# RWKV recurrence: eight blocks of two heads, taken in four pairs

## The chip, the cores and the metric

One core of a Trainium2 chip runs the whole program in one launch. The metric is the device time of one execution in microseconds. TensorE (PE in the profile, its weight loads PEld) multiplies, VectorE (DVE) and ScalarE (ACT) copy and compute, GpSimd (POOL) fills buffers and takes powers, and SyncE (SP) issues the loads.

## The reference

A network of two blocks on 256 positions of width 1024. The change touches one of its parts, the RWKV time mix of the first layer:

```python
def wkv7_scan(r, decay, k, v, a, b):
    def step(S, inp):
        r_t, w_t, k_t, v_t, a_t, b_t = inp
        sa = jnp.einsum('bhij,bhj->bhi', S, a_t)
        S = S * w_t[:, :, None, :] + sa[..., None] * b_t[:, :, None, :] + v_t[..., None] * k_t[:, :, None, :]
        return S, jnp.einsum('bhij,bhj->bhi', S, r_t)
    _, y = lax.scan(step, S0, xs)

def rwkv7_time_mix(...):
    ...
    y = wkv7_scan(heads(r), heads(decay), heads(k), heads(v), -kk, kk * a_h)
    mean = jnp.mean(y, axis=-1, keepdims=True)
    var = jnp.mean(jnp.square(y - mean), axis=-1, keepdims=True)
    y = ((y - mean) * lax.rsqrt(var + RWKV_LN_EPS)).reshape(B, T, C) * ln_g + ln_b
    bonus = jnp.sum(heads(r) * heads(k) * r_k, axis=-1, keepdims=True)
    y = y + (bonus * heads(v)).reshape(B, T, C)
    return (y.astype(h.dtype) * g) @ w_o
```

There are 16 heads of width 64. Everything else (feed-forward layers, differential attention, the second block with its expert lookup) is the same in both kernels.

## The kernel before

Activations lie transposed, 128 channels on the partitions and 256 positions in the free dimension, in eight column blocks `d`. One `d` holds two heads of 64 channels; below, "head" means one `d`. The scan over 256 steps is done in two chunks of 128 positions, each as a triangular system.

Around the change the work goes so. While the value projection runs (`rproj`, whose matmuls are `mm<-xs,raw`), DVE solves small triangular systems (L659, L661), and `prep` builds for heads 0 and 1 what the chains need: four transposes into one bank (`tr`), copied to `tk`, and four grams (`gr`, L243) of 64 rows each, copied under a mask into `gm` (L1215). Then class `Wkv` runs one generator `head(d)` for each head. It copies the solved 32x32 blocks into block-diagonal buffers `xb` (L1234 on DVE for the first two heads, L1236 on ACT after that; eight copies a head), multiplies `lp` and `lx` to an inverse (`zt` copied under a mask at L1249, the result `x3`, shown as `x`, at L1256), and runs two chunks. A chunk is a chain in one bank `ch`: PE starts it (`ch<-tk,gm`), DVE copies half to `rt` (L1271), PE multiplies by the inverse (`ch<-rt,x`), DVE copies to `ut` (L1280), PE (`ch<-ut,xs`), DVE `rt` (L1287), PE, DVE `ut`, then the output (`ch<-gm`) that ACT copies to `y` (L1303), and after the first chunk the state `s0` (`sp`, L1302). The head's tail normalises `y` (`mn`, L1314, `smp`, POOL's power L336, four `yn` at L1323 to L1326), and `last_proj` multiplies by the output projection as heads become ready. Its first three blocks are added to `x` at L391; five more follow.

Three sets of `gm`, `zt` and `tk` exist (`nb` is 3), so head `d` waits until head `d-3` has ended. PSUM's banks are rings of `wk` (four), `sm` (two) and `mm` (two); the grams use `sm`, as does the statistics bank `smp`; `tr`, `lp`, `lx`, `ch`, `sp` and `mn` use `wk`. `stagger` starts a generator every five rounds, at most five at once. A scheduler under the language then sets each engine's order; each engine runs its own in order.

Of the kernel before, what the change touches and what calls it, by code (L numbers as in the profile page):

```python
# [173 lines left out]
class Net:  # L174
# [219 lines left out]
    def transposes(self, ins, out):  # L394
        p = self.wkt("tr")
# [764 lines left out]
class Wkv:  # L1160
    def __init__(self, net, ar, bt, kt, gg, vf, tab, xd, xtd, gram):
        self.net = net
        self.a = (ar, bt, kt, gg, vf, tab, xd, xtd, gram)
        self.gms, self.tks, self.zts, self.x1s, self.pre = [], [], [], [], {}
# [9 lines left out]
    def buffers(self, pool, s):  # L1174
        nc = self.net.nc
        gm = pool.tile([128, 4, 384], F32, name=f"gm{s}")
        z = pool.tile([128, 4, 128], F32, name=f"zt{s}")
        nc.gpsimd.memset(gm, 0.0)
        nc.gpsimd.tensor_copy(z, self.net.ident[:, None, :].to_broadcast([128, 4, 128]))
        self.gms.append(gm)  # L1180
        self.zts.append(z)
        self.tks.append(pool.tile([128, 4, 128], F32, name=f"tk{s}"))

    def diag(self, pool, s):
        x1 = pool.tile([128, 2, 4, 128], F32, name=f"xb{s}")
        self.net.nc.gpsimd.memset(x1, 0.0)
# [12 lines left out]

    def prep(self, d):  # L1200
# [167 lines left out]
```

## Time and profile before

| | |
|---|---|
| median of three runs | 2212.38 us (2208.43 to 2221.66) |
| profiled execution | 2211.49 us, span 2209.7 us |
| PE, PEld busy | 2169.1, 2032.6 us (98%, 92%) |
| DVE, ACT, POOL busy | 1533.2, 1116.3, 78.0 us |
| mean granted TensorE clock | 0.994 |
| first `lp` of the recurrence | 348.05 us into the span |
| last `y` copy | 454.44 us |
| first residual copy after the output projection (L391) | 465.33 us |

The recurrence proper is the stretch from 348 to 465 us, some 5% of the span. Busy PE is no measure of its work, since matmuls are pipelined and their ends are modelled; how soon the next instruction starts says more.

### The profile page before, as it was taken

The numbers are of one execution on the slowest core, as the hardware profiler recorded it, in microseconds if no ns is written. First come the engines' busy times: TensorE is split into PE (matmuls) and PEld (weight loads), VectorE is DVE, ScalarE is ACT, GpSimd is POOL, SyncE is SP. The second block draws the span as 40 slices with busy tenths as digits, with TensorE's granted clock in tenths as the row PEclk, the third lists the DMA queues.
The fourth block names the chain that finished last, engine by engine and source line by source line (L and its number), as shares of the span: only waits on it lengthen the run. The fifth ranks groups of instructions, "written<-read, shape, count | busy, mean of one in ns | idle before, by whom it ended". The sixth has DMA issues, their size and how long they took to land.

```text
span 2209.7 us, 40311 instructions
## 1 busy us (share of the span) xinstructions
PE 2169.1 (98%) x16048; PEld 2032.6 (92%) x16048; DVE 1533.2 (69%) x2982; ACT 1116.3 (51%) x2070; POOL 78.0 (4%) x109
## 2 busy tenths in 40 slices
PE   8999999989999999999999999999999999999999
PEld 8998777779999999989999999999999999888887
DVE  6665695666666666486666767999489985666665
ACT  5443633344454444475445654444576654554554
POOL 0000040000000000020001000000000000000000
PEclk9999999999999999999999999999999999999999
DMA  6564331135565555435565445555544345555554
GB/s 214 183 180 141 117 105 39 39 105 182 180 183 179 167 179 178 136 112 189 183 180 179 136 145 172 163 172 176 192 138 131 130 145 187 192 192 195 194 192 152
DMA packets 98589, 351.06 MB, mean 159 GB/s; under 512 B 10944, under 2 KB 12480, under 8 KB 98272
## 3 DMA queue, kind: packets, MB, share of 16 engines
q1 hardware_dynamic: 98400, 348.48, 49.2%
q8 instruction: 126, 2.06, 0.4%
q14 instruction: 63, 0.52, 0.1%
HBM read 347.38 MB, written 1.05 MB: 158 GB/s over the span
## 4 chain that ended last, share of the span: by engine, by line
PE 48%; DVE 5%; issue 1%; ACT 0%; DMA 0%; POOLq 0%; POOL 0%; ACTq 0%
PE mm L243 28%; PE y L243 16%; PE pg L243 3%; DVE wl L258 2%; DVE dm L1130 1%; DVE ex L1135 0%; PE sc L243 0%; DVE dm L1133 0%; PE po L243 0%; DVE v L1098 0%; PE tr L762 0%; PE psc L243 0%; DMA raw<-in_p_u_dram 0%; DVE si L1100 0%; PE smp L243 0%
## 5 line engine op out<-in xcount | busy, mean ns | idle before, releaser
L243 PE MATMUL mm<-xs,wh 128*128 128x256 f32 x6304 | 1160.4, 286 | 14.0 <-ACT wh L255 6.8
L243 PEld LDWEIGHTS mm<-xs,wh 128*128 128x128 f32 x6304 | 988.3, 193 | 20.4 <-ACT wh L255 6.8
L258 DVE TENSOR_TENSOR wl<-raw,wh 128x1024 fp32r<-128x1024 f32 (+1 forms) x633 | 765.9, 1210 | 328.0 <-ACT wh L255 327.0
L255 ACT ACTIVATE wh<-raw 128x1024 fp32r<-128x1024 f32 (+1 forms) x633 | 660.5, 1044 | 594.7 <-PE mm L243 472.5
L243 PE MATMUL mm<-xs,wl 128*128 128x256 f32 x3152 | 896.6, 285 | 2.0 <-DVE wl L258 2.0
L243 PEld LDWEIGHTS mm<-xs,wl 128*128 128x128 f32 x3152 | 607.2, 193 | 2.9 <-DVE wl L258 2.9
L243 PE MATMUL y<-wh,cs 128*128 128x512 f32 x1024 | 274.0, 390 | 0.0
L243 PE MATMUL mm<-hh,wh 128*128 128x256 f32 x1408 | 250.1, 281 | 0.0
L243 PEld LDWEIGHTS y<-wh,cs 128*128 128x128 f32 x1024 | 192.3, 188 | 39.6
L243 PEld LDWEIGHTS mm<-hh,wh 128*128 128x128 f32 x1408 | 215.9, 188 | 0.0
L243 PE MATMUL mm<-hh,wl 128*128 128x256 f32 x704 | 198.1, 281 | 0.0
L243 PE MATMUL y<-wl,cs 128*128 128x512 f32 x512 | 157.8, 390 | 0.0
L243 PEld LDWEIGHTS mm<-hh,wl 128*128 128x128 f32 x704 | 132.6, 188 | 0.0
L243 PE MATMUL mm<-xs,raw 128*128 128x256 f32 x512 | 126.1, 394 | 2.5 <-DVE xs L490 2.5
L243 PEld LDWEIGHTS y<-wl,cs 128*128 128x128 f32 x512 | 96.2, 188 | 20.0
L306 ACT ACTIVATE cs<-ga 128x256 fp32r<-128x256 f32 x103 | 43.0, 418 | 136.9 <-PE y L243 136.7
L243 PEld LDWEIGHTS mm<-xs,raw 128*128 128x128 f32 x512 | 96.2, 197 | 16.9 <-DVE xs L490 2.9
L420 DVE TENSOR_TENSOR gu<-mm,rstd 128x512 f32<-128x512 f32 x88 | 60.8, 691 | 44.4 <-PE mm L243 44.2
L306 ACT ACTIVATE hh<-hv 128x256 fp32r<-128x256 f32 x88 | 36.6, 416 | 104.6 <-DVE hv L425 104.6
L307 DVE TENSOR_TENSOR cs<-ga,cs 128x256 fp32r<-128x256 f32 x103 | 43.8, 426 | 55.1 <-ACT cs L306 55.1
L1045 DVE TENSOR_SCALAR ohb<-iota,xT 128x128 f32<-128x128 f32 x192 | 59.5, 343 | 15.3 <-PE pg L243 13.9
L243 PE MATMUL pg<-ohb,xT 128*128 128x128 f32 x512 | 65.9, 276 | 0.0
(320 smaller groups left out, 1883.9 us busy)
## 6 DMA issues: line engine op xcount, KB each, us to landing
raw<-in_ffn_in_dram SPq DMA_DIRECT2D x176, 512.0 KB, 3.8
raw<-in_p_u_dram SPq DMA_DIRECT2D x128, 512.0 KB, 3.7
raw<-in_p_v_dram SPq DMA_DIRECT2D x128, 512.0 KB, 4.3
raw<-in_ffn_out_dram SPq DMA_DIRECT2D x64, 512.0 KB, 3.6
raw<-in_w_in_dram SPq DMA_DIRECT2D x34, 512.0 KB, 3.7
raw<-in_ffn_out_dram SPq DMA_DIRECT2D x32, 384.0 KB, 3.3
raw<-in_w_rkv_dram SPq DMA_DIRECT2D x24, 512.0 KB, 3.7
raw<-in_w_kv_dram SPq DMA_DIRECT2D x16, 512.0 KB, 3.7
```

The costliest lines, as they stand in the source:

```text
L243: self.nc.tensor.matmul(out, lhsT, rhs, start=start, stop=stop, skip_group_check=True)
L255: hi = nc.scalar.activation(fh[:rows, :w], raw[:rows, :w], AF.Copy)
L258: lo = nc.vector.tensor_tensor(fl[:rows, :w], raw[:rows, :w], fh[:rows, :w].bitcast(F32), op=ALU.subtract)
L306: nc.scalar.activation(dst[rows, :T], src, AF.Copy)
L307: nc.vector.tensor_tensor(dst[rows, T:], src, dst[rows, :T].bitcast(F32), op=ALU.subtract)
L420: nc.vector.tensor_tensor(t, p.rearrange("p (a b) -> p a b", a=2), box["r"][:, None, :].to_broadcast([128, 2, T]), op=ALU.mult)
L1045: nc.vector.tensor_scalar(b, iota, itp[:, 1, t:t + 1], itp[:, 2, t:t + 1], op0=ALU.is_equal, op1=ALU.mult)
L1130: nc.vector.tensor_tensor(m, iota[:, None, :50].to_broadcast([128, 16, 50]), bf[:, h, :, None].to_broadcast([128, 16, 50]), op=ALU.is_equal)
```

## The change

Two heads go through one generator `pair(n)`. Each chain step writes both heads' columns of one bank (`p` the first 256 columns, `pu` the other), and one DVE copy of 256 columns moves them. The state's matmuls and the output reuse the same bank, and `sp` is gone. `front(d)` builds a head's inverse, now without waiting for an earlier head's end; `tail(d)` is the old tail, run for both heads in step. In `prep` the two halves' grams alternate in two banks. The inverse is kept as its two diagonal blocks of 64 (`x3` has 64 columns, two ACT copies). There are two `zt` and four `gm` and `tk`; the last two `tk` lie in a buffer `spare` taken from the ring of split weights. `tr`, `lp` and `lx` use `sm`.

```diff
-    def transposes(self, ins, out):
-        p = self.wkt("tr")
+    def transposes(self, ins, out, bank=None):
+        p = (bank or self.wkt)("tr")
...
     def run(self, yo, w_o):
-        for s in range(2, EVERY["nb"]):
-            self.buffers(lp, s)
+        spare = net.wp.tile([128, 8, 128], F32, name="spare", tag="wh")
+        for s in range(2, 4):
+            self.buffers(lp, s, spare[:, 4 * s - 8:4 * s - 4])
-        self.x3 = lambda: lp.tile([128, 4, 128], F32, name="x3", bufs=3)
+        self.x3 = lambda: lp.tile([128, 4, 64], F32, name="x3", bufs=4)
-        stagger([self.head(d) for d in range(8)] + [net.last_proj(w_o, yo, self.ready, True)], EVERY["wkv"], EVERY["width"])
+        stagger([self.pair(n) for n in range(4)] + [net.last_proj(w_o, yo, self.ready, True)], EVERY["wkv"], EVERY["width"])
     def prep(self, d):
-        yield from net.transposes([vf[:, d, :128], vf[:, d, 128:], bt[:, d, 0], kt[:, d, 0]], f2(tk))
-        for q in range(4):
-            hh, c = q // 2, q % 2
-            hs = slice(64 * hh, 64 * hh + 64)
-            p = net.smt("gr")
-            net.mm(p[:, :128], bt[hs, d, c], ar[hs, d, c, 1], True, False)
-            net.mm(p[:, 128:384], kt[hs, d, c], ar[hs, d, c].rearrange("p a b -> p (a b)"), False, True)
-            yield
-            nc.vector.copy_predicated(gm[:, q], gmask, p[:, :384])
+        yield from net.transposes([vf[:, d, :128], vf[:, d, 128:], bt[:, d, 0], kt[:, d, 0]], f2(tk), net.smt)
+        for c in range(2):
+            ps = [net.smt("gr") for hh in range(2)]
+            for part in range(2):
+                for hh, p in enumerate(ps):
+                    hs = slice(64 * hh, 64 * hh + 64)
+                    if part == 0:
+                        net.mm(p[:, :128], bt[hs, d, c], ar[hs, d, c, 1], True, False)
+                    else:
+                        net.mm(p[:, 128:384], kt[hs, d, c], ar[hs, d, c].rearrange("p a b -> p (a b)"), False, True)
+            yield
+            for hh, p in enumerate(ps):
+                nc.vector.copy_predicated(gm[:, 2 * hh + c], gmask, p[:, :384])
...
+    def front(self, d):
...
+        p = net.smt("lp")
...
+        p = net.smt("lx")
...
+        xc = self.x3()
+        for lo in (0, 64):
+            rows = slice(lo, lo + 64)
+            nc.scalar.activation(xc[rows], p[rows].rearrange("p (a b) -> p a b", a=4)[:, :, rows], AF.Copy)
+        self.solved.add(d)
+        yield
+        while d >= 4 and d - 4 not in self.ended:
+            yield
+        if d not in self.pre:
+            yield from self.prep(d)
...
+    def pair(self, n):
+        ds = (2 * n, 2 * n + 1)
+        live = [self.front(d) for d in ds]
+        while live:
+            live = [g for g in live if next(g, live) is not live]
+            yield
...
+            bank = net.wkt("ch")
+            p, pu = bank[:, :T], bank[:, T:]
...
+            rt = net.tmp("rt")
             nc.vector.tensor_copy(rt[:64], p[:64])
...
             for lo in (0, 64):
                 rows = slice(lo, lo + 64)
-                for hh in range(2):
-                    cols = slice(64 * hh, 64 * hh + 64)
-                    net.mm(pu[rows, cols], xc[rows, 2 * hh + c, rows], rt[rows, cols], hh == 0, hh == 1)
+                for e in range(2):
+                    for hh in range(2):
+                        net.mm(pu[rows, col(e, hh)], xcs[e][rows, 2 * hh + c], rt[rows, col(e, hh)], e == 0 and hh == 0, True)
...
+        live = [self.tail(d, y) for d, y in zip(ds, ys)]
+        while live:
+            live = [g for g in live if next(g, live) is not live]
+            yield
```

Up to the second half of the value projection, and from the last blocks of the output projection on, the order of every engine is the same in both kernels. Between them it differs; three places follow. In the names, a number belongs to one buffer.

ACT just after the value projection's last copies, before the change:

```order
L526 ACTIVATE vf<-mm 128x256 x4
L1236 ACTIVATE xb_3495<-hd 32x4x32 x4
L1256 ACTIVATE x_3727<-lx 128x512
...
L1236 ACTIVATE xb_3502<-hd 32x4x32 x4
L1256 ACTIVATE x_3760<-lx 128x512
L1236 ACTIVATE xb_3502<-hd 32x4x32 x2
L399 ACTIVATE tk_3707<-tr 128x512
```

And after it, up to the copies of the second pair's transposes into `spare`:

```order
L526 ACTIVATE vf<-mm 128x256 x4
L1239 ACTIVATE xb_3495<-hd 32x4x32 x4
L1239 ACTIVATE xb_3502<-hd 32x4x32 x4
L1256 ACTIVATE x_3746<-lx 64x256 x2
L1239 ACTIVATE xb_3495<-hd 32x4x32 x2
L1256 ACTIVATE x_3749<-lx 64x256 x2
...
L1256 ACTIVATE x_3805<-lx 64x256 x2
...
L1256 ACTIVATE x_3808<-lx 64x256 x2
...
L399 ACTIVATE spare<-tr 128x512 x2
```

The first inverse copies moved from behind four `xb` copies to behind eight, and the transposes' copies stand behind 32.

PE at the same place, before:

```order
L243 MATMUL lp<-xb_3495,xs 128x128 x4
L243 MATMUL gr<-ar,bt 128x128
L243 MATMUL gr<-ar,kt 128x256
...
L243 MATMUL lx<-xb_3495,zt_3491 128x128 x4
L243 MATMUL ch<-tk_3494,gm_3490 128x64 x2
L243 MATMUL lp<-xb_3502,xs 128x128 x4
L243 MATMUL ch<-rt,x_3727 64x64 x2
```

And after:

```order
L243 MATMUL ch<-tk_3492,gm_3490 128x64 x2
L243 MATMUL ch<-tk_3499,gm_3497 128x64 x2
L243 MATMUL lp<-xb_3495,xs 128x128 x4
L243 MATMUL lp<-xb_3502,xs 128x128 x4
L243 MATMUL ch<-rt,x_3746 64x64 x2
L243 MATMUL ch<-rt,x_3749 64x64 x2
L243 MATMUL lx<-xb_3495,zt_3493 128x128 x4
L243 MATMUL lx<-xb_3502,zt_3500 128x128 x4
L243 MATMUL ch<-ut,xs 64x64 x4
L397 MATMUL tr<-base,vf 128x128 x2
```

The next pair's `lp` and `tr` now stand between the chain's steps, where grams and the other head's steps stood.

DVE where a tail's `yn` meet a chain's copies, before (one head's tail):

```order
L340 COPY re<-sm 128x256
L1215 COPY_PREDICATED gm_3703<-rtab,gr 128x384
L1280 COPY ut<-ch 64x128 x2
...
L1302 SCALAR_TENSOR_TENSOR s_4207<-sp,dcy,base 128x128
L1323 TENSOR_TENSOR yn<-yc,smp 128x256
L1324 TENSOR_SCALAR yn<-yn,vec 128x256
L1249 COPY_PREDICATED zt_3704<-rtab,lp 128x512
L1325 TENSOR_TENSOR yn<-yn,bv 128x256
L1287 COPY rt<-ch 64x128
L1326 TENSOR_TENSOR yn<-yn,gg 128x256
```

And after (the tails of pair 0, the first chain copies of pair 2):

```order
L333 TENSOR_SCALAR sm<-smp 128x4 x2
L340 COPY re<-sm 128x256 x2
L1291 COPY rt<-ch 64x256
L1356 TENSOR_TENSOR yn<-yc,smp 128x256 x2
L1357 TENSOR_SCALAR yn<-yn,vec 128x256 x2
L1358 TENSOR_TENSOR yn<-yn,bv 128x256 x2
L1359 TENSOR_TENSOR yn<-yn,gg 128x256 x2
L1300 COPY ut<-ch 64x256
```

A chain's `rt` now stands behind both `re` of two tails, and its `ut` behind all eight `yn`.

## Rows read from the trace of the kernel before

**Rows 1.** The page, busy time and share of the span by engine.

```profile
PE 2169.1 (98%) x16048; PEld 2032.6 (92%) x16048; DVE 1533.2 (69%) x2982; ACT 1116.3 (51%) x2070; POOL 78.0 (4%) x109
```

**Rows 2.** Busy time by window: window, length, then each engine, clock, DMA.

```profile
348.00:378.00 30.00, 30.00 (x243) 23.50 (x243) 15.07 (x40) 15.28 (x36) 1.18 (x1) 1.00 0.06 19
...
454.00:460.00 6.00, 2.36 (x13) 1.64 (x13) 2.26 (x8) 0.69 (x2) 1.89 (x2) 0.97 0.01 3
460.00:467.00 7.00, 6.03 (x26) 5.08 (x27) 4.67 (x12) 3.36 (x6) 0.00 (x0) 0.54 0.00 0
467.00:482.00 15.00, 15.00 (x128) 15.00 (x127) 13.71 (x24) 10.34 (x19) 0.00 (x0) 1.00 0.60 190
```

**Rows 3.** PE's waits from 348 to 453: total us, times, longest.

```profile
PE smp L243 <- ACT sq L1319: 0.7, 1, 0.7
...
PE ch L243 <- DVE ut L1280: 0.2, 1, 0.2
```

**Rows 4.** Timeline of weight loads around grams: start, us, engine, line.

```profile
328.60 0.29 PEld L243 LDWEIGHTS gr<-ar,bt 64*128 64x128 f32 x2 [0.33 <-issue]
...
330.11 0.19 PEld L243 LDWEIGHTS mm<-xs,raw 128*128 128x128 f32 x1 [0.33 <-issue]
...
333.76 0.31 PEld L243 LDWEIGHTS gr<-ar,bt 64*128 64x128 f32 x4 [0.33 <-issue]
...
334.62 0.19 PEld L243 LDWEIGHTS mm<-xs,raw 128*128 128x128 f32 x1 [0.33 <-ACT vf L526]
...
338.44 0.29 PEld L243 LDWEIGHTS gr<-ar,bt 64*128 64x128 f32 x2 [0.50 <-DVE gm L1215]
...
340.20 3.32 PEld L243 LDWEIGHTS mm<-xs,raw 128*128 128x128 f32 x16 [0.33 <-issue]
...
343.86 0.29 PEld L243 LDWEIGHTS gr<-ar,bt 64*128 64x128 f32 x2 [0.33 <-DVE gm L1215]
...
344.70 0.19 PEld L243 LDWEIGHTS mm<-xs,raw 128*128 128x128 f32 x1 [0.33 <-ACT vf L526]
```

**Rows 5.** Timeline of weight loads at the recurrence's start.

```profile
348.05 1.08 PEld L243 LDWEIGHTS lp<-xb,xs 128*128 128x128 f32 x8
...
352.75 0.30 PEld L243 LDWEIGHTS ch<-rt,x 64*64 64x64 f32 x4
...
353.12 0.18 PEld L243 LDWEIGHTS gr<-ar,kt 64*128 64x128 f32 x1
```

**Rows 6.** Groups from 348 to 455: count, busy us, mean ns, idle before.

```profile
L1236 ACT ACTIVATE xb<-hd 32x128 f32<-32x128 f32 x48 | 20.3, 422 | 3.9 <-PE lp L243 2.9
...
L1215 DVE COPY_PREDICATED gm<-rtab,gr 128x384 f32<-128x384 uint32 x24 | 14.1, 586 | 8.0 <-PE gr L243 7.6
...
L1280 DVE COPY ut<-ch 64x128 f32<-64x128 f32 x32 | 9.2, 286 | 4.6 <-PE ch L243 3.9
...
L336 POOL TENSOR_TENSOR sm<-sm,mhalf 128x4 f32<-128x4 f32 x7 | 7.5, 1071 | 110.3 <-DVE sm L333 110.3
...
L1256 ACT ACTIVATE x<-lx 128x512 f32<-128x512 f32 x8 | 4.8, 597 | 12.6 <-PE lx L243 12.5
...
L1323 DVE TENSOR_TENSOR yn<-yc,smp 128x256 f32<-128x256 f32 x6 | 2.5, 410 | 0.6 <-PE smp L345 0.6
```

**Rows 7.** Timeline of ACT: a copy of 256 columns, four `xb` copies.

```profile
328.71 0.38 ACT L526 ACTIVATE vf<-mm 128x256 f32<-128x256 f32 x1 [1.53 <-PE mm L243]
...
349.40 1.76 ACT L1236 ACTIVATE xb<-hd 32x128 f32<-32x128 f32 x4 [0.56 <-PE lp L243]
```

**Rows 8.** Timeline of the last head's tail.

```profile
454.44 0.28 ACT L1303 ACTIVATE y<-ch 128x128 f32<-128x128 f32 x1 [1.71 <-PE ch L243]
...
461.13 0.41 DVE L1324 TENSOR_SCALAR yn<-yn,vec 128x256 f32<-128x256 f32 x1
461.46 0.42 DVE L307 TENSOR_TENSOR xs<-yn,xs 128x256 fp32r<-128x256 f32 x1
...
465.33 0.76 DVE L391 SCALAR_TENSOR_TENSOR xT<-mm,xT 128x256 f32<-128x256 f32 x2 [1.75 <-PE mm L243]
```

More of the change, by code (lines that the diff above doesn't have):

```diff
@@ L1172, in open, with buffers, diag @@
             self.diag(rg, s)
[L1174 removed]
+    def buffers(self, pool, s, tk=None):
+        gm = pool.tile([128, 4, 384], F32, name=f"gm{s}")
+        self.net.nc.gpsimd.memset(gm, 0.0)
+        self.gms.append(gm)
+        self.tks.append(pool.tile([128, 4, 128], F32, name=f"tk{s}") if tk is None else tk)
+    def diag(self, pool, s):
         nc = self.net.nc
[L1176 removed]
         z = pool.tile([128, 4, 128], F32, name=f"zt{s}")
[L1178 removed]
         nc.gpsimd.tensor_copy(z, self.net.ident[:, None, :].to_broadcast([128, 4, 128]))
[L1180 removed]
         self.zts.append(z)
[L1182 to L1184 removed]
         x1 = pool.tile([128, 2, 4, 128], F32, name=f"xb{s}")
[L1186 removed]
+        nc.gpsimd.memset(x1, 0.0)
         self.x1s.append(x1)
@@ L1237, in head @@
         yield
-        while d >= EVERY["nb"] and d - EVERY["nb"] not in self.ended:
-            yield
-        if d not in self.pre:
-            yield from self.prep(d)
-        gm, tk = self.pre[d]
-        z = self.zts[d % EVERY["nb"]]
-        p = net.wkt("lp")
+        z = self.zts[d % 2]
+        p = net.smt("lp")
         for q in range(4):
@@ L1282, in head @@
                 if lo == 0:
-                    for hh in range(2):
-                        cols = slice(64 * hh, 64 * hh + 64)
-                        net.mm(p[64:, cols], gram[:64, d, 2 * hh + c, 64:], ut[:64, cols], False, hh == 1)
+                    for e, d in enumerate(ds):
+                        for hh in range(2):
+                            net.mm(p[64:, col(e, hh)], gram[:64, d, 2 * hh + c, 64:], ut[:64, col(e, hh)], False, True)
                     yield
@@ L1289, in head, with tail @@
             if c == 0:
-                psn = net.wkt("sp")[:, :128]
-                net.mm(psn, tk[:, 2], ut, True, False)
-                net.mm(psn, tk[:, 3], tk[:, 0], False, True)
-            for hh in range(2):
-                hs = slice(64 * hh, 64 * hh + 64)
-                net.mm(o[hs], ut[:, hs], gm[:, 2 * hh + c, :128], False, False)
-                net.mm(o[hs], tk[:, c, hs], gm[:, 2 * hh + c, T:], False, c == 0)
-            if c:
-                net.mm(o, s0, ar[:, d, 1, 1], False, True)
+                for e in range(2):
+                    net.mm(pu[:, own(e)], tks[e][:, 2], ut[:, own(e)], e == 0, False)
+                    net.mm(pu[:, own(e)], tks[e][:, 3], tks[e][:, 0], False, True)
+            for e, d in enumerate(ds):
+                for hh in range(2):
+                    hs = slice(64 * hh, 64 * hh + 64)
+                    net.mm(p[hs, own(e)], ut[:, col(e, hh)], gms[e][:, 2 * hh + c, :128], c == 1 and e == 0, False)
+                    net.mm(p[hs, own(e)], tks[e][:, c, hs], gms[e][:, 2 * hh + c, T:], False, c == 0)
+                if c:
+                    net.mm(p[:, own(e)], s0[:, own(e)], ar[:, d, 1, 1], False, True)
             yield
             if c == 0:
-                s0 = net.tmp("s0", 128)
-                nc.vector.scalar_tensor_tensor(s0, psn, net.dcy[:, d:d + 1], net.bones, op0=ALU.mult, op1=ALU.mult)
-            nc.scalar.activation(y[:, c * 128:(c + 1) * 128], o, AF.Copy)
-            yield
-        self.ended.add(d)
+                s0 = net.tmp("s0")
+                for e, d in enumerate(ds):
+                    nc.vector.scalar_tensor_tensor(s0[:, own(e)], pu[:, own(e)], net.dcy[:, d:d + 1], net.bones, op0=ALU.mult, op1=ALU.mult)
+            for e in range(2):
+                nc.scalar.activation(ys[e][:, c * 128:(c + 1) * 128], p[:, own(e)], AF.Copy)
+            yield
+        self.ended.update(ds)
+        live = [self.tail(d, y) for d, y in zip(ds, ys)]
+        while live:
+            live = [g for g in live if next(g, live) is not live]
+            yield
+    def tail(self, d, y):
+        net = self.net
+        nc, vec = net.nc, net.v
+        ar, bt, kt, gg, vf, tab, xd, xtd, gram = self.a
+        v2 = lambda a: a.rearrange("p (c t) -> p c t", c=2)
         rk = net.tmp("rk")
```

40 lines of the change are left out of this document (21 added, 19 removed).

## The prediction

> **What bounds the kernel now.** I read the page's busy times first [rows 1]: TensorE (PE) is busy 98% of 2209.7 us. So the question is what PE does in the stretch that the change touches. The two programs' orders agree on every engine outside the recurrence, so the whole effect is won or lost between the first grams (324 us) and the end of the output projection's first three blocks, whose residual copy L391 starts at 465.33 [rows 8].
>
> The window from 348 to 378 [rows 2] shows PE without a gap while its weight loads (PEld) fill 23.5 of 30 us, and DVE and ACT are half idle. The waits [rows 3] are four, together 1.7 us in 105. Yet this is not PE at its peak. A gram alone takes 0.84 us up to the next instruction [rows 4], from 343.86 to 344.70, though its four loads are issued within 0.33: the matmul that follows has another tile shape and starts only when the gram is through. One head's `ch<-rt` takes 0.37 [rows 5], from 352.75 to 353.12, 0.22 for four records and 0.15 for that changeover. So what ends last in this stretch is PE's own work and its changeovers; three heads interleave well enough that no copy is waited for.
>
> **The change, part by part.** Times below count from the first `lp` (348.05 before [rows 5]); the last `y` copy stands at 106.4 (454.44 [rows 8]).
>
> *Grams.* Two grams on opposite halves took 0.86 us together [rows 4], from 333.76 to 334.62, two on the same half 1.51 [rows 4], from 328.60 to 330.11. Of the 32 grams 24 lie after the first `lp`. Before, nearly all stand alone: 24 x 0.84 = 20.2. After, they stand in opposite halves: 12 x 0.86 = 10.3. PE saves 9.9. If the halves did not overlap, a pair would cost 1.51 and the saving would be 2.1.
>
> *Chain steps for two heads.* `ch<-rt` goes from 32 x 0.37 = 11.8 to 16 x (0.44 + 0.15) = 9.4, saving 2.4; `ch<-ut,xs` from 16 to 8 such blocks, saving 1.2. The other joined blocks (`ch<-tk,gm`, the state's two matmuls, `ch<-gm`, `mn`, `smp`) lose about 24 changeovers of 0.15 to 0.3: 4.8 at 0.2.
>
> *The output projection.* Its steps for heads 4 and 5 ran before the last `y`; now they stand behind it, 2 x 9 matmuls of 0.117 (15 us for 128 [rows 2]) = 2.1 moved into the tail, where PE has room.
>
> PE's work up to the last `y` thus falls by 9.9 + 2.4 + 1.2 + 4.8 + 2.1 = 20.4.
>
> *Copies.* DVE makes 32 copies of 256 columns for 64 of 128: 32 x 0.41 (the 256-column `yn<-yc,smp`) against 64 x 0.286 [rows 6], 5 us less. DVE has room [rows 2], so this is worth nothing by itself; each hop of a chain gets 0.12 longer. ACT's inverse copy becomes two of 64x256: 16 x 0.38 (as `vf`, 256 columns [rows 7]) for 8 x 0.60 [rows 6], 1.3 more. POOL's fourth `gm` memset replaces a `zt` copy some 30 us before its use: nothing.
>
> *What is added: waits.* Grams, transposes, `lp` and `lx` now all use the two "sm" banks, with the tails' `smp`; before, the last three had four "wk" banks. PE takes instructions in the order listed, so one bank that is late stops all behind it. I walked the new order with the durations of the rows:
>
> 1. Start. Before the first inverse copy `x`, ACT has eight `xb` copies instead of four. One takes 0.42 to 0.44 [rows 6, 7], so `x` of head 1 ends at 7.0; the second pair's `lp` needs those banks and stands ahead of `ch<-rt` on PE. The chain's first `ch<-rt` comes at 8.2 (4.7 before: 352.75). PE idles 1.7.
> 2. Up to the copies of the second pair's transposes ACT has 32 `xb` (14.0), eight halves of `x` (3.0) and two `spare` (1.2): it works without a break from 1.1 to 19.3. PE's transposes `tr` wait for banks that ACT frees at 14.0 and 15.7, and the following `lp` for one at 18.9: idle 2.7 + 0.6 + 1.4 = 4.7.
> 3. Eight grams of pair 1 through two banks, each freed by a 0.586 us copy [rows 6], with other DVE work between: PE could do them in 3.4, they take until 27.5. Idle 2.4.
> 4. Both pairs in flight (29 to 43): 0.5. Pair 1's second chunk alone, four hops of PE, DVE, PE: 2.3.
> 5. Pair 2's preparation with both tails of pair 0 in the two banks: DVE's `rt` stands behind two `re`, each behind a POOL power of 1.07 [rows 6], and `ut` behind eight `yn` (8 x 0.38 = 3.0, between a length of 0.41 and 0.34 from start to start [rows 8]). Before, the four `yn` of one head were spread among the chains' copies. Idle 7.3 up to 79.7.
> 6. Pair 1's tails the same way ahead of both chains' `ut`: 3.1. Last chunk alone: 1.2.
>
> Sum of waits: 1.7 + 4.7 + 2.4 + 0.5 + 2.3 + 7.3 + 3.1 + 1.2 = 23.2. Last `y`: 106.4 - 20.4 - 1.7 (the waits of before) + 23.2 = 107.5. Counting the new order's PE blocks from the bottom instead gives 81 of work and 23.2 of waits: 104.3. I take 106, 0.4 earlier.
>
> *The v projection ahead.* Four paired gram blocks (3.4) for eight grams that cost 0.84 twice, 1.51, 0.86 and 1.76 (338.44 to 340.20), 5.8 in all [rows 4], and one changeover fewer (0.3): 2.7 saved; but the seventh and eighth solve steps on DVE now wait for a gram, and PE then waits about 1.0 for DVE to free a bank. Net 1.7 earlier.
>
> *The tail.* From the last `y` to the residual took 10.9 us for one head [rows 8], from 454.44 to 465.33. Two heads in lockstep need 14.2: the fourth projection weight's cast stands ahead of `y` on ACT because its buffer was the spare (0.5), two `y` and two `mn` run one after the other (0.7), and eight `yn` instead of four stand between the statistics and the last matmuls (1.5 more), with a second `yc`, `bv` and POOL power (0.6). Plus 3.3.
>
> Sum: -0.4 - 1.7 + 3.3 = +1.2 us. The profiled execution had 2211.5 (span 2209.7), the median of the three runs is 2212.4; I put the sum on the median and round down a little: **2213**.
>
> A page against a row: the row of two halves says 0.86 for a pair of grams. The Trainium skill, "TensorEngine Tiling (Array Packing)", section "PSUM Bottleneck", says that tiling speeds up TensorE but not the emptying of PSUM. By that rule alone the 24 grams would go at DVE's pace of 0.586 each, 14.1 instead of 10.3, and the sum would be +5; the walk has this wait already where nothing else fills it (3 and 5).
>
> **The rivals.**
> *The waits are smaller than walked (2202).* The new order was laid out with its waits in view (single chain steps stand between grams), and before, the order met only 1.7 us of them. Against it: ACT's backlog is 18 us of counted copies. If half of the first three waits and of the fifth are not there, 8 to 11 us go.
> *Nearly all waits are absent (2190).* All of 20 saved. The ACT count speaks against it.
> *The halves don't overlap.* If the grams' bank waits pull the halves apart, 12 x (1.51 - 0.86) = 7.8 comes back: 2221. The grams of pairs 2 and 3 stand two by two in the order, which speaks against it; pair 1's are split by chain steps.
> *Slower: the clock.* Before, the granted clock stays at 1.00 through the recurrence and falls in 454 to 460, where PEld was busy 1.64 of 6 us; in 460 to 467 it is 0.54, that is 1.2 GHz for most of it [rows 2]. The new order has thin stretches in four places (11 to 19, 59 to 67, 82 to 87 and the tail), PEld about half busy. Each drop costs at most the work done in some 7 us once more, 2 to 3.5 us; two more give 2218. If the clock stays low through waits 2 to 6, some 20 us of PE work double and the kernel ends at 2233; it decides against the change from the point where the thin stretches run together. The Trainium skill, "TensorE: Matmul & The Clock Gate", section "Part 1: The HAM clock gate", says that the throttled state is the default and activity releases it; the drop at 460 agrees.
>
> **How the numbers follow.** Forecast as summed, 2213: 0.54 (its own range 2206 to 2220). Smaller waits: 0.18. No waits: 0.08. Halves apart: 0.06. Clock: 0.14, of it 0.06 beyond 2234. One per cent (22 us) is about what a measurement of this kernel can tell from no change, and a fifth of the stretch touched. Faster by more: 0.08 (no waits); slower by more: 0.07 (the clock, and 0.01 for halves apart with a slow clock); within: 0.85. The range leaves out the last part of either side: 2199 to 2227.
>
> **What would show it.** In the new profile: two grams in about 0.86 us; PE waits of some 20 us in the recurrence where there were 1.7, with "sm" users (`tr`, `lp`, `gr`) waiting for ACT `x` and DVE `gm`, and `ch` for DVE `ut`; ACT busy without a break for 18 us after the first `lp`; last `y` near 452; residual near 466. Wrong it would be if PE's waits stay under 8 us (then some 2198) or PEclk shows several half-speed stretches between 355 and 440.

## The result, and the profile after

The changed kernel took 2227.65 us in the median of 11 runs (2218.81 to 2238.29), the kernel before 2212.51 beside it: a ratio of 1.0073, 95% interval 1.0059 to 1.0087. That is 15 us slower, clear of the interval, though within the 1% that the prediction called no change; it is 0.65 us above the range forecast and 14.7 above the number. The profiled execution of the changed kernel had 2234.0 us, that of before 2211.5; the difference of 22.5 is found whole between the v projection and the residual: the first `lp` comes 1.2 later (349.21 for 348.05), the last `y` 16.2 later from there (122.6 for 106.4), and the tail, from the row of the last `y` to the residual, takes 16.0 where it took 10.9.

The page's busy line of the changed kernel, against [rows 1]:

```profile
PE 2179.4 (98%) x16048; PEld 2047.0 (92%) x16048; DVE 1527.4 (68%) x2950; ACT 1115.3 (50%) x2078; POOL 78.3 (4%) x109
```

PE is busy 10 us longer with the same number of instructions, though the change was to save it 20. The cause shows in the next view. Busy time by window of the changed kernel, columns as in [rows 2] (window, length, PE, PEld, DVE, ACT, POOL, granted clock, DMA):

```profile
349.00:363.00 14.00, 10.81 (x91) 9.84 (x89) 4.06 (x7) 12.16 (x30) 0.00 (x0) 1.00 0.11 40
363.00:371.00 8.00, 7.32 (x38) 6.32 (x39) 0.59 (x2) 5.91 (x15) 0.00 (x0) 0.57 0.00 0
371.00:393.00 22.00, 21.88 (x191) 18.17 (x190) 11.09 (x22) 8.45 (x23) 0.00 (x0) 1.00 0.01 2
393.00:418.00 25.00, 20.50 (x160) 16.01 (x158) 13.91 (x31) 7.61 (x17) 2.01 (x2) 1.00 0.19 64
418.00:429.00 11.00, 11.00 (x50) 9.11 (x47) 5.88 (x17) 2.64 (x6) 0.00 (x0) 0.53 0.00 0
429.00:445.00 16.00, 13.27 (x108) 10.54 (x108) 10.10 (x28) 1.20 (x4) 2.01 (x2) 1.00 0.00 1
445.00:459.00 14.00, 14.00 (x92) 12.43 (x92) 2.37 (x6) 0.45 (x2) 0.00 (x0) 0.51 0.00 1
459.00:466.00 7.00, 6.03 (x51) 5.09 (x48) 4.65 (x14) 1.28 (x4) 1.52 (x2) 0.99 0.00 1
466.00:477.00 11.00, 10.40 (x51) 8.31 (x52) 6.71 (x18) 2.00 (x5) 0.46 (x1) 0.54 0.09 29
477.00:483.00 6.00, 2.75 (x22) 2.19 (x20) 3.68 (x14) 0.83 (x2) 1.98 (x2) 0.99 0.10 36
483.00:490.00 7.00, 5.60 (x25) 5.31 (x26) 3.96 (x11) 3.78 (x8) 0.00 (x0) 0.52 0.00 0
```

The rows alternate. A window in which PE waits (10.8 busy of 14, 20.5 of 25, 13.3 of 16, 2.75 of 6) is followed by one in which the granted clock is close to 0.5, that is 1.2 GHz. Before, in these stretches, this happened once, at the end of the last tail [rows 2]; from the end of the first row there up to the last `y` the clock stayed at 1.00:

```profile
378.00:454.00 76.00, 74.24 (x578) 57.95 (x576) 50.68 (x134) 26.78 (x59) 5.47 (x6) 1.00 0.09 29
```

Counted from the five low rows as twice (1 - clock) times the length, the clock was low for 6.9 + 10.3 + 13.7 + 10.1 + 6.7 = 47.7 us, which is 24 us of PE work not done. Over the whole span, (1 - clock) times the span is 33.5 us in this execution and 13.3 in that of before: 20 of the 22.5 us between them. In the low rows PE is nearly always busy: the page's 98% tells nothing of it.

PE's waits from the first `lp` to the last `y` (total us, times, longest), against [rows 3]:

```profile
PE tr L397 <- ACT x L1256: 2.6, 1, 2.6
PE mm L243 <- ACT xs L306: 1.7, 1, 1.7
PE ch L243 <- DVE ut L1300: 1.7, 3, 0.6
PE ch L243 <- DVE s L1324: 1.3, 3, 0.4
PE lp L243 <- ACT x L1256: 1.3, 2, 0.8
PE smp L345 <- DVE re L340: 1.2, 2, 0.8
PE ch L243 <- DVE rt L1307: 1.0, 2, 0.5
PE gr L243 <- ACT tk L399: 0.9, 1, 0.9
PE gr L243 <- DVE gm L1219: 0.2, 1, 0.2
```

Together 11.9, for the 23.2 forecast. Of these, 7.8 are waits that the prediction named (`tr` and `lp` for ACT, `ch` for `ut` and `rt`, `smp` for `re`); the 1.7 of `mm` for `xs` is not among them, and `gr` waits only 0.2 for `gm`. Those in its second half are shorter than forecast. That a PE at half speed is itself late there, and so waits less, is likely but no run shows it apart.

The recurrence's start, weight loads of the changed kernel, against [rows 5]:

```profile
349.21 1.97 PEld L243 LDWEIGHTS lp<-xb,xs 128*128 128x128 f32 x16
...
354.99 0.97 PEld L243 LDWEIGHTS lp<-xb,xs 128*128 128x128 f32 x8 [0.93 <-ACT x L1256]
356.67 0.97 PEld L243 LDWEIGHTS lp<-xb,xs 128*128 128x128 f32 x8 [0.72 <-ACT x L1256]
357.76 0.54 PEld L243 LDWEIGHTS ch<-rt,x 64*64 64x64 f32 x8
```

The first `ch<-rt` is 8.55 behind the first `lp` (forecast 8.2), after two waits of 1.65 together (forecast 1.7). ACT there, against [rows 7]:

```profile
350.57 3.58 ACT L1239 ACTIVATE xb<-hd 32x128 f32<-32x128 f32 x8 [0.56 <-PE lp L243]
354.17 0.77 ACT L1256 ACTIVATE x<-lx 64x256 f32<-64x256 f32 x2
...
365.33 2.63 ACT L1239 ACTIVATE xb<-hd 32x128 f32<-32x128 f32 x6
367.99 1.09 ACT L399 ACTIVATE spare<-tr 128x512 f32<-128x512 f32 x2
370.90 1.30 ACT L1239 ACTIVATE xb<-hd 32x128 f32<-32x128 f32 x3 [1.82 <-PE lp L243]
```

ACT works without a break up to 369.08, 19.9 behind the first `lp` (forecast 19.3).

Two grams of pair 1 (weight loads), against [rows 4]:

```profile
372.83 0.29 PEld L243 LDWEIGHTS gr<-ar,bt 64*128 64x128 f32 x2 [0.17 <-issue]
373.05 0.30 PEld L243 LDWEIGHTS gr<-ar,kt 64*128 64x128 f32 x2
373.29 0.29 PEld L243 LDWEIGHTS gr<-ar,bt 64*128 64x128 f32 x2
373.50 0.30 PEld L243 LDWEIGHTS gr<-ar,kt 64*128 64x128 f32 x2
374.13 0.20 PEld L243 LDWEIGHTS ch<-gm,ut 128*64 128x64 f32 x4 [0.33 <-issue]
```

Two halves on PE at once show as one row of four loads (`x4`), as at 333.76 before. Here the rows read `bt`, `kt`, `bt`, `kt` with two loads each: one half after the other, 1.30 us from 372.83 to 374.13, not 0.86. Behind the first `lp` no block of two grams took 0.86: two whose rows are merged in part took 1.08 and 1.13, the others 1.23 to 1.32 at full clock. Three of the four pairs in the v projection do overlap (`x4`, 0.85 to 0.86); the fourth first waits for a bank:

```profile
331.80 0.48 PE L243 MATMUL gr<-ar,bt 64*128 64x128 f32 x2 [1.94 <-DVE gm L1219]
```

The end, the last `y` and the first residual, against [rows 8]:

```profile
471.85 0.43 ACT L1326 ACTIVATE y<-ch 128x128 f32<-128x128 f32 x2
```

```profile
487.83 1.09 DVE L391 SCALAR_TENSOR_TENSOR xT<-mm,xT 128x256 f32<-128x256 f32 x3 [2.90 <-PE mm L243]
```

The single operations cost what was forecast: groups of the changed kernel (count, busy, mean ns), against [rows 6]:

```profile
L1219 DVE COPY_PREDICATED gm<-rtab,gr 128x384 f32<-128x384 uint32 x24 | 12.8, 578 | 6.3 <-PE gr L243 6.3
...
L1300 DVE COPY ut<-ch 64x256 f32<-64x256 f32 x16 | 6.6, 418 | 11.8 <-PE ch L243 11.8
...
L1256 ACT ACTIVATE x<-lx 64x256 f32<-64x256 f32 x16 | 6.0, 378 | 4.2 <-PE ch L243 4.0
```

### The profile page after: what moved, and what is told of

It is laid out like the page before. It is cut to its first block, busy times and chain, and to the rows that moved or that the text cites. A ratio compares the mean times of both kernels' runs of the same rounds, so it can differ in the third digit from the quotient of the medians.

```text
span 2232.2 us, 40293 instructions
## 1 busy us (share of the span) xinstructions
PE 2179.4 (98%) x16048; PEld 2047.0 (92%) x16048; DVE 1527.4 (68%) x2950; ACT 1115.3 (50%) x2078; POOL 78.3 (4%) x109
## 4 chain that ended last, share of the span: by engine, by line
PE 51%; DVE 2%; issue 0%; ACT 0%; DMA 0%; POOLq 0%; POOL 0%; ACTq 0%
PE mm L243 31%; PE y L243 16%; PE pg L243 3%; DVE wl L258 1%; PE psc L243 0%; PE sc L243 0%; DVE dm L1130 0%; PE po L243 0%; DVE ex L1135 0%; PE tr L762 0%; DVE dm L1133 0%; DMA raw<-in_p_u_dram 0%; PE smp L243 0%; ACT wh L255 0%; DVE bi L1100 0%
## 5 line engine op out<-in xcount | busy, mean ns | idle before, releaser
L243 PE MATMUL mm<-xs,wh 128*128 128x256 f32 x6304 | 1164.5, 287 | 17.1 <-ACT wh L255 7.0
L1045 DVE TENSOR_SCALAR ohb<-iota,xT 128x128 f32<-128x128 f32 x192 | 59.6, 344 | 15.3 <-PE pg L243 13.9
```

The lines of the kernel that those rows point to most:

```text
L243: self.nc.tensor.matmul(out, lhsT, rhs, start=start, stop=stop, skip_group_check=True)
L1045: nc.vector.tensor_scalar(b, iota, itp[:, 1, t:t + 1], itp[:, 2, t:t + 1], op0=ALU.is_equal, op1=ALU.mult)
```

## The experiments

Two theories stand against each other. By the **clock theory** the walk of the prediction was right, and the loss is PE at 1.2 GHz behind the thin stretches. By the **waits theory** the waits themselves cost the 15 us, and a low clock comes where PE would have waited anyway.

One program, with one order of instructions, differs from run to run mainly in its clock. The 11 runs of the changed kernel lie on a line of 18.9 us for each 0.010 of mean granted clock (2218.8 at 0.991, 2238.3 at 0.981), 101 runs of the kernel before on one of 19.9. So the table gives, beside the median, the **time at full clock**: the time less (1 - clock) times the span, for each run, then the median. It takes off too much where PE would have waited anyway. The clock is on record to 0.001, which is 2.2 us of the span, so differences of a microsecond or two between such times say nothing.

| kernel | median us (runs) | ratio to the kernel before, run beside it, 95% | median clock | at full clock |
|---|---|---|---|---|
| before | 2212.0 (101) | | 0.994 | 2199 |
| changed | 2227.65 (11) | 1.0073 [1.0059, 1.0087] | 0.987 | 2199 |
| b_grams | 2211.03 (10) | 0.9992 [0.9977, 1.0008] | 0.993 | 2195 |
| a_wk | 2229.66 (4) | 1.0070 [1.0043, 1.0096] | 0.984 | 2193 |
| a_tails | 2222.32 (8) | 1.0059 [1.0034, 1.0084] | 0.990 | 2200 |
| a_fill | 2228.00 (8) | 1.0060 [1.0040, 1.0080] | 0.993 | 2213 |
| a_xb | 2228.31 (4) | 1.0089 [1.0069, 1.0109] | 0.987 | 2198 |
| a_fillh | 2226.92 (4) | 1.0075 [1.0058, 1.0092] | 0.990 | 2205 |
| a_comb | 2216.96 (9) | 1.0017 [1.0004, 1.0030] | 0.990 | 2194 |
| a_xt | 2217.93 (7) | 1.0026 [1.0007, 1.0046] | 0.991 | 2198 |
| b_f | 2211.99 (12) | 1.0007 [0.9993, 1.0021] | 0.996 | 2202 |
| b_gf | 2210.12 (12) | 0.9992 [0.9976, 1.0009] | 0.995 | 2200 |
| a_cf | 2215.74 (12) | 1.0015 [1.0002, 1.0028] | 0.992 | 2197 |
| a_gr0 | 2239.36 (4) | 1.0124 [1.0090, 1.0158] | 0.985 | 2206 |
| a_gwk | 2216.57 (10) | 1.0018 [1.0004, 1.0033] | 0.989 | 2193 |
| a_gwxt | 2209.78 (12) | 0.9986 [0.9975, 0.9996] | 0.991 | 2190 |
| a_gwxtf | 2208.41 (12) | 0.9982 [0.9971, 0.9993] | 0.993 | 2193 |

At full clock the changed kernel and the one before can't be told apart. The kernel before was run beside every experiment, with medians from 2211.7 to 2212.6. The rest of the section asks whether that reading holds when single parts are moved. The scheduler can lay out a new order for an edit, so an edit's worth is that of the part together with its order.

**b_grams**: the kernel before, with the new gram loop in `prep` alone.

> The kernel before with one part of the change alone: in prep the two halves' grams alternate in two banks, and heads still go singly, with tr, lp and lx on the wk banks. Both theories take the 9.9 us of work that the prediction put on this (24 grams of 0.84 us alone against 12 pairs of 0.86). Clock theory (the changed kernel loses its time because a PE thinned out by waits falls to 1.2 GHz): with the heads single nothing thins PE, the clock stays near 0.994 and the time is some 2200 to 2206. Waits theory (two gram banks taken at once are freed too late, and PE waits for gm copies what it saves): 2209 to 2214.

At full clock it gains 4 us, less than half of the 9.9, and the median gains 1. The clock fell from 0.994 to 0.993: low stretches appeared 52 us behind the first `lp` and in the v projection, where none was before. Neither number expected came out; work taken from PE is partly paid back.

**a_wk**:

```diff
-        yield from net.transposes([...], f2(tk), net.smt)
+        yield from net.transposes([...], f2(tk))
-        p = net.smt("lp")
+        p = net.wkt("lp")
-        p = net.smt("lx")
+        p = net.wkt("lx")
```

> The changed kernel with tr, lp and lx back on the four wk banks, so that only grams and statistics use the two sm banks. It removes the waits of tr, lp and gr for ACT's copies at offsets 11 to 19 (4.7 us by the walk) and eases the later ones. Waits theory: the median falls by these 5 to 7 us and the half-speed stretches matter no more than before: 2220 to 2223. Clock theory: one or two of the seven half-speed stretches between 360 and 490 us go too, each with 2 to 4 us: 2214 to 2220, granted clock above 0.988. If both stay as they are, neither the banks nor ACT's backlog made the loss: 2226 to 2230.

Both theories missed; the median lies in the last range named (2226 to 2230). At full clock 6 us are gone (2193), and all of it went to the clock (0.984): the first drop, 15 us behind the first `lp`, now lasted 20 us. The edit did not remove the waits that it was meant to remove: in the first 20 us behind the first `lp` PE waited 4.4 us (2.0 of it `tr` for ACT's `x`), in the changed kernel 3.9.

**a_tails**:

```diff
+        if n < 2:
+            for d, y in zip(ds, ys):
+                yield from self.tail(d, y)
+            return
         live = [self.tail(d, y) for d, y in zip(ds, ys)]
```

> The changed kernel with the two tails of pair 0, and the two of pair 1, one after the other instead of in step, so that the next pair's rt and ut stand behind one tail's copies and not behind two. The half-speed stretches at offsets 69 to 79 and 96 to 110 follow the waits 5 and 6 that the prediction put on these tails. Waits theory: up to half of 7.3 + 3.1 us goes, 2222 to 2225, with the clock as it was. Clock theory: if PE stays fed there, two or three half-speed stretches of 3.4 us each go as well, 2214 to 2221; if the clock record is as in the changed kernel, the time is too (2225 to 2230).

Four runs at 0.991 took 2219.8 to 2220.4 us, three at 0.981 to 0.983 took 2233.8 to 2234.9, the eighth 2224.2 at 0.990. One program and one order, 14 us apart with its clock: the order's waits alone don't explain that, though the median lies in the waits theory's range, 1 us above the clock theory's. At full clock nothing is gained (2200), so the tails in step cost nothing by themselves there. In the profiled execution, at 0.991, the drops of 10 and 14 us at 418 and 445 had given way to two of 3.4 and 6.8; the changed kernel's profile is of an execution at 0.985, so part of that can be chance.

**a_fill**: matmuls whose results nobody reads.

```diff
+    def fill(self, rows, w, x, n):
+        for k in range(n):
+            fb = self.net.wkt("fill")
+            self.net.mm(fb[rows, :x.shape[-1]], w, x, True, True)
...
+                self.fill(rows, xcs[0][rows, 0], rt[rows], 1)
...
+                    self.fill(slice(64, 128), gram[:64, ds[0], 0, 64:], ut[:64], 1)
...
+        self.fill(slice(0, 128), net.bones, sq, 3)
```

> The changed kernel with matmuls added whose results nobody reads: one of 256 columns after every ch<-rt and every ch<-ut step (24) and three behind the statistics of each tail (24), in a wk bank of their own. No wait is removed, and some 20 us of work is added to PE, part of it where PE would wait for DVE or ACT. Clock theory: PE no longer thins out, the half-speed time in the recurrence falls from 48 us to under 25, the granted clock is 0.990 or more, and the time is 2210 to 2224 in spite of the added work. Waits theory: the added work stands in the chains' way and the time is 2230 to 2245, whatever the clock.

Five of the stretches above, with 48 matmuls more (the first `lp` comes 2.2 us later here):

```profile
363.00:371.00 8.00, 6.21 (x40) 4.62 (x39) 0.85 (x2) 7.61 (x19) 0.00 (x0) 0.79 0.00 0
...
418.00:429.00 11.00, 10.19 (x50) 7.28 (x51) 5.86 (x17) 1.55 (x4) 1.12 (x2) 0.69 0.00 0
...
445.00:459.00 14.00, 14.00 (x122) 10.99 (x122) 6.11 (x17) 1.14 (x4) 0.00 (x0) 1.00 0.00 1
...
466.00:477.00 11.00, 10.91 (x82) 8.86 (x82) 8.24 (x23) 2.42 (x6) 1.98 (x2) 1.00 0.09 24
477.00:483.00 6.00, 4.94 (x30) 3.81 (x29) 3.44 (x13) 0.42 (x1) 1.98 (x2) 1.00 0.11 46
483.00:490.00 7.00, 5.71 (x43) 5.34 (x44) 5.23 (x13) 5.12 (x11) 0.00 (x0) 1.00 0.10 22
```

Where the changed kernel had 0.51, 0.54 and 0.52, the clock is 1.00, though no wait was removed. Where it had 0.57 and 0.53 the drops are shorter, and a new one of 3.4 us stands at 404: from the first `lp` to the residual the clock is low for 13.7 us instead of 47.7. So work in place of waiting holds the clock up. The run is not quite the changed kernel and added work alone, since the scheduler also moved some grams and `mn` steps on PE; the tails below are the cleaner case. The added work costs 14 us at full clock, the clock gives about as much back, and the median (2228.0) lies between the two expectations: it is no remedy.

**a_xb**: `if d < 2:` becomes `if d < 2 or src is xtd:`, so that half of the block copies go to DVE.

> The changed kernel with the four xtd block copies of every head on DVE, so that ACT has 16 xb copies ahead of the second pair's transposes' copies instead of 32. Waits theory: the walk's wait 2 goes (4.7 us), the granted clock doesn't matter, 2222 to 2224. Clock theory: the thin stretch at offsets 11 to 19 is the first that drops PE to 1.2 GHz; without it that drop of 3 to 7 us goes as well, but the later drops stay: 2218 to 2223, clock 0.987 to 0.990. Taken with its own clock (time less half the half-speed time of all stretches) it should stand some 4 to 5 us under the changed kernel; if it doesn't, ACT's backlog was not the wait.

The backlog is gone:

```profile
351.68 2.66 ACT L1239 ACTIVATE xb<-hd 32x128 f32<-32x128 f32 x6
354.73 0.77 ACT L1256 ACTIVATE x<-lx 64x256 f32<-64x256 f32 x2 [0.39 <-PE lx L243]
...
359.88 1.09 ACT L399 ACTIVATE spare<-tr 128x512 f32<-128x512 f32 x2
```

The copies into `spare` start 14.0 behind the first `lp` (345.87) instead of 18.8, and the first `y` at 26.2 instead of 31.4. That is the 4.7 of wait 2. The time does not show it: four runs from 2216.8 at 0.991 to 2234.7 at 0.981, as wide as the changed kernel's own, and 2198 at full clock, 1 us under the changed kernel where 4 to 5 were expected. So the backlog was the wait, as the trace shows, but removing it did not bring its time. The drop that the clock theory tied to it is gone: the profiles of the seven changed kernels without this edit (the changed kernel itself, a_fill, a_fillh, a_wk, a_tails, a_gwk, a_gr0) all have a drop that begins 14 to 17 us behind the first `lp`, those of the six with it (a_xb, a_xt, a_comb, a_cf, a_gwxt, a_gwxtf) have none before 21 us.

**a_xt** and **a_comb**: the edits of a_xb and a_tails together, without and with that of a_wk.

> The changed kernel with two edits: the xtd block copies on DVE and the tails of pairs 0 and 1 one after the other; tr, lp and lx stay on the sm banks. The tails alone gave 2219.8 in five of eight runs at a clock of 0.991 and 2234 in three at 0.983. Clock theory: with the first thin stretch gone too, 0.991 to 0.993 and 2210 to 2217, in runs at a lower clock up to 2230. Waits theory: the two edits' waits add up, 2222.3 less 4.7: 2217 to 2219 whatever the clock.

> The changed kernel with three edits at once: tr, lp and lx on the wk banks, the xtd block copies on DVE, and the tails of pairs 0 and 1 one after the other. Time less clock losses was 2199 for the changed kernel, 2193 with the wk banks alone; with ACT's backlog gone I expect 2187 to 2191. Waits theory: the granted clock is as before the change (0.994), and the time is 2201 to 2205, faster than both kernels. Clock theory: a PE with less to do and the same chains to wait for falls to 1.2 GHz as often, the clock is 0.985 to 0.990, and most of the gain is paid back: 2209 to 2222.

a_xt came to 2217.9, from 2214.6 at 0.992 to 2220.5 at 0.990: in the waits theory's range and 1 us above the clock theory's, but its runs follow their clock. a_comb tells more: 2194 at full clock (a little worse than hoped), and the median at 2217.0, inside the clock theory's range and 12 us above the other's.

**a_fillh**: as a_fill, 128 columns wide.

> The same added matmuls as in the filled kernel, at the same places, but 128 columns wide instead of 256: about half the added work, some 10 us, and half the activity in the thin stretches. Time less clock losses was 2214 with 256 columns and 2199 without, so it should be near 2206 here under either theory. Clock theory: what is paid to the clock lies between the two, 10 to 25 us, so 2217 to 2228, and over the runs the time follows the granted clock by 17 to 22 us for each 0.010. Waits theory: the time follows the added work alone, 2228 plus or minus 2, with no such slope.

2205 at full clock, as expected, and 0.990 between the two. The ranges of the theories overlap here, and the slope over four runs was 8.6 where the clock theory expected 17 to 22, so it adds little.

**b_f**, **b_gf**, **a_cf**: matmuls only where PE waits in the last tail, in the kernel before, in b_grams and (there for both heads of the last pair) in a_comb. `fill(x, n)` multiplies `bones` by `x`; `more` is called behind the two statistics matmuls.

```diff
         net.mm(p[:, T:], net.bones, rk, False, True)
+        if d == 7:
+            self.fill(rk, 2)
...
-        rb = yield from net.gstat_g(sq, net.bmask2, 2, 1.0 / 64, 64e-5)
+        rb = yield from net.gstat_g(sq, net.bmask2, 2, 1.0 / 64, 64e-5, more=lambda: d == 7 and self.fill(sq, 3))
+        if d == 7:
+            self.fill(sq, 1)
```

> The kernel before with six matmuls of 256 columns added in the last head's tail, where PE waits for DVE, POOL and ACT (two behind mn, three behind the statistics, one behind the transposed powers); nobody reads them, and no wait is removed. Before, the clock fell to 1.2 GHz for 6.8 us there, which costs up to 3.4 us of PE work. Clock theory: that half-speed stretch is gone or half as long, the granted clock rises from 0.994 to 0.995 to 0.997, and the time falls by 1 to 3 us although work is added: 2209 to 2211. Waits theory: nothing (2212) or slower by what sticks out of the gaps, up to 1.5 us.

> The kernel with only the grams' halves alternating, and the same six matmuls added in the last head's tail. It had 2211.0 at a clock of 0.993, with a half-speed stretch of 10.2 us from offset 110; time less clock losses was 2195. Clock theory: without that stretch 3 to 5 us go, 2206 to 2209, which would beat both kernels by some 0.2%. Waits theory: 2211 to 2213.

> The changed kernel with the three edits (wk banks, xtd copies on DVE, tails of pairs 0 and 1 in turn), which had 2217.0 at a clock of 0.990, and eight matmuls of 256 columns added in the tails of the last pair, where PE waits 1.3, 0.5 and 2.6 us. Half-speed stretches of 3.4 to 6.8 us stood at offsets 100 and 114. Clock theory: the second goes, 2 to 4 us, 2213 to 2215 at 0.991 to 0.993; the first stays. Waits theory: 2217 to 2219.

The tail of b_f, in the windows of [rows 2]:

```profile
454.00:460.00 6.00, 4.99 (x32) 3.96 (x32) 2.41 (x8) 0.69 (x2) 1.72 (x2) 1.00 0.01 3
460.00:467.00 7.00, 5.06 (x30) 3.52 (x29) 4.85 (x13) 2.75 (x5) 0.43 (x1) 1.00 0.00 0
```

With 19 records more in the first window (the execution runs 0.9 us later there) the clock holds at 1.00, where it was 0.97 and 0.54. The same came out in all four kernels filled in this way (a_gwxtf follows below): the tail's drop, 6.8 us in the kernel before, a_comb and a_gwxt and 10.2 in b_grams, is gone, while PE's order in the recurrence is otherwise the same. Nothing but matmuls of no use was added, so for the tail it is shown that the drop comes from PE standing idle there. But the tail only went from 10.9 to 10.3 us, and the median did not move, as the waits theory had it. In the last tail PE waits for DVE and ACT so much that its speed hardly counts; the clock theory's 1 to 3 us were too much. a_cf's tail went from 14.2 to 12.9 us and its median down by 1.2, which missed both ranges and is within the spread of the runs; b_gf (0.9992, between its two ranges) can't be told from no change. In the four the time at full clock rises by 2 to 5 us while the medians fall by 0 to 1.4: it charges a low clock in a tail some 3 us too much, so the changed kernel's 2199 may be a few us too low.

**a_gr0** and **a_gwk**: the changed kernel with the old gram loop, and with `net.wkt("gr")` for `net.smt("gr")`.

> The changed kernel with the old gram loop: each half's two matmuls together in one bank, copied before the next half's. If the prediction's term is right in it (12 pairs at 0.86 us, 9.9 us of work saved), undoing it adds 8 to 10 us to the time less clock losses: 2207 to 2209 instead of 2199. If the two sm banks come free one at a time and pull the halves apart (the rival of the prediction at 2221), the alternation saves hardly anything there and undoing it changes nothing: 2197 to 2202 less clock losses, 2222 to 2232 with them, the clock 0.984 to 0.989 as in the changed kernel.

> The changed kernel with the grams' banks from the four wk banks instead of the two sm banks; tr, lp, lx and the statistics keep the sm banks. By the order six of the twelve pairs of halves now stand two and two. If bank waits pull the halves apart in the changed kernel, these six take 0.86 us instead of 1.3 and the waits for ACT's and DVE's copies fall: time less clock losses 2193 to 2197 instead of 2199. Clock theory: part of that is paid back, 2217 to 2226 at 0.985 to 0.990. If the halves overlapped already: 2199 less clock losses and 2225 to 2230.

Undoing the alternation costs 7 us at full clock and 12 in the median, so it does save work, about two thirds of the 9.9; the gram blocks behind the first `lp` take 23.3 us in its profile, part of it at half speed, for 17.0 in the changed kernel. Banks from the larger ring give 6 at full clock and 11 in the median. Grams of a_gwk:

```profile
368.88 0.30 PEld L243 LDWEIGHTS gr<-ar,bt 64*128 64x128 f32 x4
369.10 0.31 PEld L243 LDWEIGHTS gr<-ar,kt 64*128 64x128 f32 x4
...
370.54 0.29 PEld L243 LDWEIGHTS gr<-ar,bt 64*128 64x128 f32 x2 [0.49 <-DVE gm L1219]
370.76 0.30 PEld L243 LDWEIGHTS gr<-ar,kt 64*128 64x128 f32 x2
```

The first two halves run at once (`x4`), later ones still wait for a `gm` copy each. Its gram blocks together took 17.1 us, part of it at half speed, as in the changed kernel, so from which users of the two rings the 6 us come was not separated.

**a_gwxt** and **a_gwxtf**: a_gwk, a_xb and a_tails together; then with six matmuls in the waits of the last pair's tails.

> The changed kernel with three edits: the grams on the wk banks (alone 2216.6, 2193 less clock losses), the xtd copies on DVE and the tails of pairs 0 and 1 in turn (these two alone 2217.9, 2198 less clock losses). Waits theory: both gains add to 2191 to 2193 less clock losses, and the time is 2204 to 2208. Clock theory: the less PE has to do between the same hops, the lower the clock: 0.989 to 0.991 and 2211 to 2217.

> The same three edits, and six matmuls of 256 columns added in the tails of the last pair, where PE waits for the powers and the last yn. Clock theory: the half-speed stretch of the tail goes, the clock is 0.991 to 0.994 and the time 2207 to 2214, 1 to 3 us under the kernel without them. Waits theory: no gain or up to 1.5 us slower than it.

a_gwxt took 2209.8: 2190 at full clock, 9 us under the kernel before, of which the clock (0.991 for 0.994) took about 6. The waits theory's range ended at 2208, the clock theory's began at 2211; it lies between them. a_gwxtf is the fastest of all at 2208.4, ratio 0.9982 [0.9971, 0.9993]; that it is faster than a_gwxt the intervals don't show, though its tail took 12.9 us for 14.2. The tail's window in a_gwxt, then in a_gwxtf, where the clock holds:

```profile
455.00:462.00 7.00, 3.49 (x16) 3.02 (x17) 4.08 (x12) 0.75 (x2) 0.95 (x1) 0.62 0.01 6
```

```profile
455.00:462.00 7.00, 5.15 (x31) 3.84 (x29) 4.33 (x13) 1.48 (x3) 1.01 (x2) 1.00 0.02 6
```

## Why the prediction was wrong

It failed at one step: the sum has no term for the clock, and the rival that has one, "Slower: the clock", was priced too low. The mechanism and its places were right: the four thin stretches it lists (11 to 19, 59 to 67, 82 to 87 and the tail) each have a drop in them or within ten microseconds behind them, and one more came at 117. Its price and its chance were wrong. It took "two more" drops of some 7 us as the likely cost, 2218, with 2233 as the outer case and 0.14 for all of it; the range ended at 2227, short of that case. Measured, in the profiled execution, were five drops of 6.7 to 13.7 us, 47.7 us at 1.2 GHz or 24 us of PE work, where before there was one of 6.8, and a sixth of 3.4 ahead of the first `lp`. The median of 2227.65 lies between its 2218 and 2233, and the profiled execution (2234.0) reached the outer case. Of its two signs of being wrong the second came: two half-speed stretches begin between 355 and 440 (at 363 and 418). The first, waits under 8 us, did not: they were 11.9. The forecast 2213 is near what the changed kernel would have at the clock of before: its line, drawn beyond its fastest run (0.991), gives 2214 at 0.994.

The other steps, one by one:

- *Grams, 9.9*: mis-sized. Before, the gram blocks behind the first `lp` took 20.8 us (forecast 20.2); in the changed kernel 17.0, not 10.3, part of it at half speed. "The grams of pairs 2 and 3 stand two by two in the order" was a misreading: rows `bt`, `kt`, `bt`, `kt` are one half after the other, and only `x2` rows are two halves at once. So the rival "the halves don't overlap" came about in part; it would have cost 7.8, and the experiments put the alternation's worth at 7 instead of 9.9. The Trainium skill, "TensorEngine Tiling (Array Packing)", section "PSUM Bottleneck", says that tiling does not speed up the emptying of PSUM. Two `gm` copies of 0.578 make 1.16, near the 1.3 that a pair took, but behind the first `lp` PE waited only 0.2 us for `gm`; the one long wait for it, 1.9 us, stands in the v projection.
- *Copies*: right, each within 0.01 us (0.418 for 0.41, 0.378 for 0.38).
- *Waits 1 and 2*: right to a few tenths (1.65 for 1.7; ACT busy to 19.9 for 19.3; `tr` 2.6 for 2.7). In a_xb wait 1 is gone, wait 2 is down to 1.1 us, and the first `y` came 5.2 earlier, for the 4.7 forecast.
- *Waits 3 to 6*: not to be read apart, because PE was at half speed in them. The last `y` stood at 122.6; the drops up to there (6.9, 10.3, 13.7 and about 6 of the fourth) leave out 18.5 us of work, and 122.6 less that is 104.1, where the count from the bottom gave 104.3 and the forecast took 106. That may be in part luck: the grams saved less than forecast and the waits were shorter, errors of opposite sign.
- *Tail, 3.3 more*: 5.1 in this execution, 9 of its 16 us at low clock. Five others (a_tails, a_xt, a_comb, a_gwk, a_gwxt), each with a drop of 6.8 us that begins in the tail, took 14.2, the number forecast. With the clock held and matmuls added, a_fill had 13.9 and a_cf 12.9.
- *v projection, 1.7 earlier*: the profile has 1.2 later, with the clock low for 3.4 us in it. Wrong by 2.9, of which the clock explains under 2. PE's wait for a bank was 1.9 where the walk had about 1.0, and the pair behind it did not overlap (1.95 us, in part at half speed, for 0.86).

What remains open: why a kernel's clock falls as often as it does, and why it is lower in one run of a program than in another. For the tail the runs show what brings it on (PE standing idle) and what keeps it off (work, even work of no use); for the first thin stretch a_xb and its like show that ACT's backlog does; for the middle ones only a_fill speaks, with its changed order. Not shown is the rule.

## What to carry to other kernels

Cost a schedule twice, once at full clock and once with PE at half speed for some 7 to 14 us behind each thin stretch (the lengths in the changed kernel's profile): a change that turns PE work into short waits can keep its time at full clock and lose 15 us to a lower one. Compare kernels by the time at full clock beside the median, with the granted clock of each run; it can show a gain that the clock hides, but no finer than a few microseconds. And read an order for pairs by its counts: two tiles run wholly at once only where their rows are merged.

## What the runs showed of the hardware

- No single wait of PE between the first `lp` and the last `y` was longer than 2.6 us, and the clock fell four times there, a fifth time in the tail. Before, it fell only in the last tail, behind waits of 0.8, 1.0 and 1.8 us. The Trainium skill, "TensorE: Matmul & The Clock Gate", section "Part 1: The HAM clock gate", says that the slow state is the default and activity lifts it. The traces agree: with matmuls of no use added, the tail's drop is gone in four kernels of four, and in a_fill the clock is 1.00 for 0.51.
- A low clock hides its own cause: PE's busy share in the window at 0.51 is 14.0 of 14, in the thin window ahead of it 13.3 of 16.
- In a tail made of waits the low clock costs little: 6.8 us of it, less the cost of the added matmuls, were worth 0.6 us for one head (b_f) and 1.3 for two (a_cf, a_gwxtf). By the 19 us for each 0.010 of mean clock it would be 2.9.
